# Up projection of a feed-forward block by seven block products instead of eight, gated activations through DRAM, and the down projection afterwards by token halves

## The chip, the cores and the metric

The kernel runs on one core of one Trainium2 chip. The metric is the device time of one execution in microseconds; the median of three runs of the kernel before is 1866.54 us (1864.61 to 1866.8).

## The reference

One layer of a hybrid causal decoder on a sequence of 1024 tokens with 1024 channels, all in float32. The token-mixing sub-layer (dilated attention and a convolution branch) and its output projection with a residual are left as they are. The change lies in the channel-mixing sub-layer:

```python
h = rms_norm(x, norm_ffn_pre)
u = h @ w_up                       # 1024 x 1024 times 1024 x 5632
u = causal_depthwise_conv(u, ffn_conv_w, ffn_conv_b)   # 3 taps along the tokens
u_gate, u_val = split(u, 2)        # 2816 channels each
f = gelu(u_gate) * u_val
y = f @ w_down                     # 1024 x 2816 times 2816 x 1024
x = x + rms_norm(y, norm_ffn_post)
```

## The kernel before, in words

All large products run on TensorE in a two-part form of float32: a value is split into a high part (`fp32r`, a ScalarE cast) and the remainder (a VectorE subtraction), and each product of two tiles is three matmuls into the same PSUM bank: high x high, high x low, low x high (`mm3`, lines 185 to 188). A matmul has a 128x128 stationary operand and 512 moving columns. Weights come from DRAM over the SP queue as 128x512 raw tiles (tag `wr`, three buffers) and are split by `split` (lines 166 and 167) into tiles `wh` and `wl` (seven buffers).

The engines work in order, each through its own list; a scheduler lays these lists out once, before the run, by a model of the times and the order of the program. Waits go through semaphores.

*Into the feed-forward part.* The output projection runs over eight token tiles in two halves (line 593). Each tile is normalised twice (with the residual between, lines 614 to 624) into rows `y`. When four tiles are there, `transposed` (lines 150 to 160) turns them on TensorE into `h2T[k, h]`: eight chunks k of 128 channels by 512 tokens, for the token half h, each as high and low part. The pool `d` has 31 buffers of 4 KB per partition for such tiles.

*Up.* `up(j)` (line 647) is called for j in 0 to 21. It makes 128 gate channels and 128 value channels of u: for both, for both token halves, over eight chunks, three matmuls, which is 2 x 2 x 8 x 3 = 96 matmuls of 512 columns into two PSUM tiles `pp` of two banks each. `conv3` (line 639) applies the three taps: one ScalarE activation and two VectorE operations of 1024 columns, reading PSUM (for j = 0 a copy in SBUF). Gelu (line 663), the product (664) and the split of f into high and low part (665, 666) follow; f stays in SBUF as `fT[j]`.

*Down.* Two blocks of f at a time are multiplied with the matching rows of `w_down` (line 687): for eight token tiles and two column halves, three matmuls for each block; the bank is then added by VectorE to an accumulator in SBUF (lines 704 and 706). The calls alternate with those of `up` (lines 711 to 716); the last call takes four blocks and ends each token tile with `finish` (line 671): the root mean square over the row, the scaling and the residual, and the store.

Of the kernel before, what the change touches and what calls it, by code (L numbers as in the profile page):

```python
# [18 lines left out]
P = 128  # L19
# [59 lines left out]
def trunk_kernel(ctx: ExitStack, tc: tile.TileContext, a, out):  # L79
# [5 lines left out]
    dpool = ctx.enter_context(tc.tile_pool(name="dpool", bufs=31))  # L85
# [44 lines left out]
    def rsqrt_of(ss, scale, eps, pool, tag, n=1):  # L130
# [17 lines left out]
        return y  # L148

# [51 lines left out]
    with ExitStack() as mix:  # L201
# [371 lines left out]
        h2T = {}  # L573
        with tc.tile_pool(name="res", bufs=1) as res:
# [18 lines left out]
            for h in range(2):  # L593
# [32 lines left out]
                for k in range(KC):  # L626
                    h2T[k, h] = dt(F32R, (P, 2, 512))
                transposed(h2, lambda k: (h2T[k, h][:, 0], h2T[k, h][:, 1]), ffn_g)


    with tc.tile_pool(name="ffn", bufs=1) as ffn:
        def h2_in(k, h):
            return h2T[k, h][:, 0], h2T[k, h][:, 1]

        acc = []
        fT = {}
        G = 2

        def conv3(ps, c, o, lo, hi):
            nc.scalar.activation(o[:, lo:hi], ps[:, lo:hi], AF.Identity, scale=ffn_w[:, c, 2:3], bias=ffn_b[:, c:c + 1])  # L640
            for k in (1, 0):
                d = 2 - k
                b = max(lo, d)
                nc.vector.scalar_tensor_tensor(o[:, b:hi], ps[:, b - d:hi - d], ffn_w[:, c, k:k + 1], o[:, b:hi],  # L644
                                               op0=ALU.mult, op1=ALU.add)

        def up(j, cuts=1):

            w = load_pair(a["w_up"][j], 4)
            pu = [pp_tile() for _ in range(2)]  # L650
            u = [ffn.tile([P, S], F32, tag="u", name="u", bufs=4) for _ in range(2)]
            fT[j] = fh, fl = dt(F32R), dt(F32R)
            n = S // cuts
            for lo in range(0, S, n):
                ts = slice(lo, lo + n)
                for c in range(2):
                    project(w, c, h2_in, pu[c], range(2 // cuts) if lo == 0 else (1,))
                    src = pu[c]
                    if j == 0:
                        src = ffn.tile([P, S], F32, tag="u", name="u", bufs=4)  # L660
                        (nc.vector.tensor_copy if c else nc.scalar.copy)(src, pu[c])
                    conv3(src, c * NF + j, u[c], lo, lo + n)
                nc.scalar.activation(u[0][:, ts], u[0][:, ts], AF.Gelu_apprx_tanh)
                nc.vector.tensor_mul(u[0][:, ts], u[0][:, ts], u[1][:, ts])
                nc.scalar.copy(fh[:, ts], u[0][:, ts])
                nc.vector.tensor_sub(fl[:, ts], u[0][:, ts], f(fh[:, ts]))

        post = ffn.tile([P, D], F32, name="post")
        nc.scalar.dma_start(post, a["norm_ffn_post"].to_broadcast((P, D)))

        def finish(T):
            o = acc[T]
            xr = ffn.tile([P, D], F32, tag="u", name="u", bufs=4)
            nc.sync.dma_start(xr, x2s[T * P:(T + 1) * P, :])
            ss = ffn.tile([P, 2], F32, tag="ss", name="ss", bufs=2)
            sq = pp_tile()
            cols = [slice(q * 512, q * 512 + 512) for q in range(2)]
            for q, cs in enumerate(cols):
                nc.scalar.activation(sq[:, cs], o[:, cs], AF.Square, accum_out=ss[:, q:q + 1])
                nc.vector.tensor_mul(o[:, cs], o[:, cs], post[:, cs])  # L680
# [6 lines left out]
        def down(ks, first=False, last=False):  # L687
            wd = {}
            for q in range(2):
                for n, k in enumerate(ks):  # L690
                    raw = wpool.tile([P, 512], F32, tag="wr", name="wr", bufs=3)
                    nc.sync.dma_start(raw, a["w_down"][k * P:(k + 1) * P, q * 512:(q + 1) * 512])
                    wd[k, q] = split(raw, (P, 512), *((ffn, "wd", 4) if n < G else (wpool, "w", 7)))
            for T in range(NT):
                ts = slice(T * P, (T + 1) * P)
                if first:
                    acc.append(dt() if T else ffn.tile([P, D], F32, name="acc0"))
                for q in range(2):
                    po = ps_tile()
                    for k in ks:  # L700
                        mm3(po, fT[k][0][:, ts], fT[k][1][:, ts], *wd[k, q], k == ks[0], k == ks[-1])
                    o = acc[T][:, q * 512:(q + 1) * 512]
                    if first:
                        nc.vector.tensor_copy(o, po)
                    else:
                        nc.vector.tensor_add(o, o, po)  # L706
                if last:
                    finish(T)

        groups = [list(range(k, k + G)) for k in range(0, NF, G)]  # L710
        for n, ks in enumerate(groups):
            for k in ks:
                up(k, 2 if k == NF - 1 else 1)
            if 0 < n < len(groups) - 1:
                down(groups[n - 1], first=n == 1)
        down(groups[-2] + groups[-1], last=True)


def _pairs(w, cols):
# [57 lines left out]
```

## Time and profile before

| | |
|---|---|
| median of three runs | 1866.54 us |
| the profiled execution, its own time | 1863.73 us |
| span of its instructions | 1862.0 us |
| TensorE busy | 1814.7 us (97%), 8392 matmuls |
| VectorE busy | 1134.3 us (61%) |
| ScalarE busy | 587.2 us (32%) |
| GpSimd busy | 57.1 us (3%) |
| moved by DMA | 143.86 MB, mean 77 GB/s |

The profile is that of one execution. PE is TensorE, PEld its weight loads, DVE VectorE, ACT ScalarE, POOL GpSimd, SP the engine whose queue issues most DMAs. Durations of matmuls are modelled and overlap: the pace is the distance from one start to the next. In a row of instruction groups stand line, engine, operation, `output<-inputs` by tile names, shapes, the count, then busy time and mean duration of one in ns, then the idle time of the engine in front of them and what ended it.

### The profile page before, as it was taken

The page shows a single profiled execution, that of the slowest core. Times are in us where ns is not written, and L with a number is a line of the kernel's source. Part 1 is how long each engine was busy: PE and PEld are TensorE (multiplying, and loading weights), DVE is VectorE, ACT ScalarE, POOL GpSimd, SP SyncE. Part 2 cuts the span into 40 slices and gives each one's busy share as a digit, 9 for nine tenths or more (in the row PEclk, how much of TensorE's full clock was granted, in tenths as well). Part 3 has the DMA queues.
Part 4 walks back from the last instruction along what each step waited for, and adds up shares of the span by engine and source line. Part 5 has one row for each costly group of instructions (what it writes and reads, how often), then busy time and mean ns, then how long its engine had stood idle before and what let it go on. Part 6 is the DMA issues. An engine that isn't in the chain of part 4 may idle for free.

```text
span 1862.0 us, 21816 instructions
## 1 busy us (share of the span) xinstructions
PE 1814.7 (97%) x8392; PEld 1524.2 (82%) x8392; DVE 1134.3 (61%) x1923; ACT 587.2 (32%) x1069; POOL 57.1 (3%) x83
## 2 busy tenths in 40 slices
PE   7899998999999999999999999999999999999997
PEld 5688898888888888888888887888888888888886
DVE  6249979258763769838654576555455545545548
ACT  6132343233313342223432344312221322222132
POOL 0000010011100000000000000000000000000000
PEclk9899999999999999999999999999999999999999
DMA  5312132122312222354231333211120211111114
GB/s 190 108 49 60 46 97 80 45 58 62 95 46 55 73 69 80 102 172 147 91 113 57 119 113 108 69 40 51 52 58 30 66 46 46 45 50 59 29 57 158
DMA packets 67079, 143.86 MB, mean 77 GB/s; under 512 B 9107, under 2 KB 11043, under 8 KB 66976
## 3 DMA queue, kind: packets, MB, share of 16 engines
q1 hardware_dynamic: 58176, 122.71, 21.4%
q0 software_dynamic: 5552, 16.19, 3.2%
q10 hardware_dynamic: 3248, 3.58, 0.6%
q8 instruction: 66, 1.08, 0.2%
q14 instruction: 37, 0.30, 0.0%
HBM read 119.23 MB, written 25.31 MB: 78 GB/s over the span
## 4 chain that ended last, share of the span: by engine, by line
PE 65%; issue 27%; DVE 2%; POOL 2%; DMA 2%; ACTq 1%; ACT 1%; SPq 0%; POOLq 0%; DVEq 0%
PE pp L186 16%; PE pp L188 16%; PE pp L187 16%; PE ps L186 2%; PE ps L188 2%; PE ps L187 2%; PE po L187 1%; PE po L186 1%; PE po L188 1%; PE pt L186 1%; PE pt L187 1%; PE pt L188 1%; ACTq L258 1%; POOL oscr L416 1%; POOL mscr L416 1%
## 5 line engine op out<-in xcount | busy, mean ns | idle before, releaser
L186 PE MATMUL pp<-d,wh 128*128 128x512 f32 x1792 | 702.3, 392 | 16.4 <-DVE d L332 15.2
L188 PE MATMUL pp<-d,wl 128*128 128x512 f32 x1792 | 701.9, 392 | 0.0
L187 PE MATMUL pp<-d,wh 128*128 128x512 f32 x1792 | 701.8, 392 | 0.0
L186 PEld LDWEIGHTS pp<-d,wh 128*128 128x128 f32 x1792 | 337.5, 188 | 86.9 <-issue 16.1
L188 PEld LDWEIGHTS pp<-d,wl 128*128 128x128 f32 x1792 | 337.6, 188 | 68.7
L187 PEld LDWEIGHTS pp<-d,wh 128*128 128x128 f32 x1792 | 337.7, 188 | 68.3
L167 DVE TENSOR_TENSOR wl<-wr,wh 128x512 fp32r<-128x512 f32 x283 | 194.2, 689 | 266.1 <-ACT wh L166 265.4
L271 DVE SCALAR_TENSOR_TENSOR acc<-cin,conv_w,acc 128x1024 f32<-128x1024 f32 x240 | 305.2, 1281 | 3.1
L166 ACT CAST wh<-wr 128x512 fp32r<-128x512 f32 x283 | 175.0, 622 | 344.9 <-PE pp L187 234.4
L644 DVE SCALAR_TENSOR_TENSOR u<-pp,ffn_w,u 128x1023 f32<-128x1023 f32 (+2 forms) x88 | 108.4, 1232 | 81.8 <-ACT u L640 80.7
L166 ACT CAST wdh<-wr 128x512 fp32r<-128x512 f32 x40 | 24.8, 622 | 184.8 <-PE ps L188 150.0
L325 PE MATMUL pp<-wh,d 128*128 128x512 f32 x192 | 79.6, 415 | 3.0 <-DVE d L332 3.0
L326 PE MATMUL pp<-wl,d 128*128 128x512 f32 x192 | 78.9, 411 | 0.0
L327 PE MATMUL pp<-wh,d 128*128 128x512 f32 x192 | 77.4, 408 | 0.0
L640 ACT ACTIVATE u<-pp,ffn_b,ffn_w 128x1024 f32<-128x1024 f32 (+1 forms) x44 | 51.3, 1166 | 77.6 <-PE pp L188 77.6
L706 DVE TENSOR_TENSOR d<-d,ps 128x512 f32<-128x512 f32 x63 | 43.2, 686 | 43.6 <-PE ps L188 43.6
L186 PE MATMUL ps<-wdh,d 128*128 128x512 f32 x160 | 62.2, 389 | 0.0
L187 PE MATMUL ps<-wdl,d 128*128 128x512 f32 x160 | 62.2, 389 | 0.0
L188 PE MATMUL ps<-wdh,d 128*128 128x512 f32 x160 | 62.2, 389 | 0.0
L380 ACT ACTIVATE pe<-sn,ml 128x128 f32<-128x128 f32 (+1 forms) x96 | 42.5, 445 | 52.7 <-DVE ml L377 52.4
L325 PEld LDWEIGHTS pp<-wh,d 128*128 128x128 f32 x192 | 53.1, 277 | 7.1 <-issue 4.0
L327 PEld LDWEIGHTS pp<-wh,d 128*128 128x128 f32 x192 | 52.9, 277 | 3.6 <-issue 0.9
(268 smaller groups left out, 2035.6 us busy)
## 6 DMA issues: line engine op xcount, KB each, us to landing
wr<-in_w_up_dram SPq DMA_DIRECT2D x88, 256.0 KB, 2.8
wr<-in_w_v_dram SPq DMA_DIRECT2D x48, 256.0 KB, 2.8
wr<-in_w_qk_dram SPq DMA_DIRECT2D x48, 256.0 KB, 2.7
wr<-in_w_down_dram SPq DMA_DIRECT2D x44, 256.0 KB, 2.9
wr<-in_w_glu_dram SPq DMA_DIRECT2D x32, 256.0 KB, 2.7
wr<-in_w_gate_dram SPq DMA_DIRECT2D x32, 256.0 KB, 3.0
ld<-oscr SPq DMA_DIRECT2D x8, 768.0 KB, 5.6
d<-in_x_dram SPq DMA_DIRECT2D x8, 512.0 KB, 5.8
```

Of the source, the lines that this page charges most:

```text
L166: nc.scalar.copy(hi, raw)
L167: nc.vector.tensor_sub(lo, raw, f(hi))
L186: nc.tensor.matmul(ps, lh, rh, start=first, stop=False)
L187: nc.tensor.matmul(ps, lh, rl, start=False, stop=False)
L188: nc.tensor.matmul(ps, ll, rh, start=False, stop=last)
L271: nc.vector.scalar_tensor_tensor(acc, cin[:, k:k + S], conv_w[:, m, k:k + 1], acc, op0=ALU.mult, op1=ALU.add)
L325: nc.tensor.matmul(ps, hTh[k][:, sl], wh, start=k == 0, stop=False)
L326: nc.tensor.matmul(ps, hTh[k][:, sl], wl, start=False, stop=False)
L327: nc.tensor.matmul(ps, hTl[k][:, sl], wh, start=False, stop=k == KC - 1)
L640: nc.scalar.activation(o[:, lo:hi], ps[:, lo:hi], AF.Identity, scale=ffn_w[:, c, 2:3], bias=ffn_b[:, c:c + 1])
L644: nc.vector.scalar_tensor_tensor(o[:, b:hi], ps[:, b - d:hi - d], ffn_w[:, c, k:k + 1], o[:, b:hi], op0=ALU.mult, op1=ALU.add)
L706: nc.vector.tensor_add(o, o, po)
```

## The change

*Operands.* The chunks k and k+4 of the normalised rows form the upper and lower half of the input (B11 and B21 for the first 512 tokens, B12 and B22 for the second). When the second half has been transposed, `strassen_rows` forms for each of four k the sums T1 = B12 - B11, T2 = B22 - T1, T3 = B22 - B12 and T4 = B21 - T2 and splits each into high and low part. B11 to B22 and T1 to T4 are 32 tiles; the pool `d` gets 32 buffers. The weights of a block are stored as four quadrants of 128 rows by 512 columns (gate and value channels by upper and lower half of the input: A11, A12, A21, A22), and GpSimd forms S1 = A21 + A22, S2 = S1 - A11, S3 = A11 - A21 and S4 = A12 - S2 of them.

*Up.* Blocks 0 and 1 run as before in eight products each (`up_plain`, first the first token half of both, then the second). Blocks 2 to 21 run as seven products of 12 matmuls (class `Seven`), in two banks of which partial sums are copied from one to the other by ScalarE (bank 1 to 2 in `fifth`, bank 2 to 1 in `second`). The loop begins the next block (`Seven(j + 1)`, `fifth`) between the products of the current one. The taps read the gate and value rows from SBUF. f is split as before, in place, and written to DRAM (`fscr`) by two DMAs per block on GpSimd's queue.

*Down.* After all up blocks, `down(0)` and `down(1)` take one token half each: four token tiles by two column halves stand in all eight PSUM banks over all 22 blocks, so nothing is added in SBUF. Each step loads f and two halves of the rows of `w_down`, so the weights are loaded and split twice. The last three blocks are taken tile by tile, with `finish` after each tile, which first copies the two banks to SBUF.

```diff
-    dpool = ctx.enter_context(tc.tile_pool(name="dpool", bufs=31))
+    dpool = ctx.enter_context(tc.tile_pool(name="dpool", bufs=32))
+    def strassen_rows(b11, b21, pt12, pt22, gain12, gain22, temp, make):
+        def parts(x):
+            t = make()
+            nc.scalar.copy(t[:, 0], x)
+            nc.vector.tensor_sub(t[:, 1], x, f(t[:, 0]))
+            return t
+        b12, b22 = temp("x12"), temp("x22")
+        nc.scalar.activation(b12, pt12, AF.Copy, scale=gain12)
+        nc.scalar.activation(b22, pt22, AF.Copy, scale=gain22)
+        out = {"B22": parts(b22), "B12": parts(b12)}
+        t1, t3, t2 = temp("x1"), temp("x3"), temp("x2")
+        nc.gpsimd.tensor_sub(t3, b22, b12)
+        nc.vector.tensor_sub(t1, b12, f(b11[:, 0]))
+        nc.vector.tensor_sub(t1, t1, f(b11[:, 1]))
+        out["T1"] = parts(t1)
+        out["T3"] = parts(t3)
+        nc.vector.tensor_sub(t2, b22, t1)
+        out["T2"] = parts(t2)
+        nc.vector.tensor_sub(t2, f(b21[:, 0]), t2)
+        nc.vector.tensor_add(t2, t2, f(b21[:, 1]))
+        return out, lambda: parts(t2)
...
+                temps = {"x12": ("xr", 0), "x22": ("xr", 1), "x1": ("oc", 0), "x2": ("oc", 1)}
+                for k in range(4):
+                    pair = [ps_tile((P, 4, P), tag) for tag in ("pt", "po")]
...
+                    wide = {"xr": nat2("xr", 2), "oc": nat2("oc", 1)}
...
+        def u_tile():
+            return ffn.tile([P, S], F32, tag="u", name="u", bufs=6)
+        def conv3(src, c):
+            o = u_tile()
+            nc.scalar.activation(o, src, AF.Identity, scale=ffn_w[:, c, 2:3], bias=ffn_b[:, c:c + 1])
             for k in (1, 0):
...
+        def gated(j, gate, val):
+            og, ov = conv3(gate, j), conv3(val, NF + j)
+            nc.scalar.activation(og, og, AF.Gelu_apprx_tanh)
+            nc.vector.tensor_mul(og, og, ov)
+            nc.scalar.copy(ov.bitcast(F32R), og)
+            nc.vector.tensor_sub(og.bitcast(F32R), og, ov)
+            for n, src in enumerate((ov, og)):
+                nc.gpsimd.dma_start(fscr[j, :, :, n, :].rearrange("h p c -> p h c"),
+                                    src.rearrange("p (h c) -> p h c", h=2))
+        def raw_tile(early=False):
+            if early:
+                return wpool.tile([P, 512], F32, tag="wr", name="wr", bufs=3)
+            return ffn.tile([P, 512], F32, tag="wq", name="wq", bufs=5)
...
+        def product(ps, w, x, first, last, open_=False):
+            for k in range(4):
+                cs = slice(k * P, k * P + P)
+                xh, xl = X[x, k][:, 0], X[x, k][:, 1]
+                for n, (wp, xp) in enumerate(((w[0], xh), (w[0], xl), (w[1], xh))):
+                    nc.tensor.matmul(ps, wp[:, cs], xp, ...)
+        def up_plain(js):
+            us = {(j, c): u_tile() for j in js for c in range(2)}
+            pps = {c: pp_tile() for c in range(2)}
+            for h in range(2):
+                for n, j in enumerate(js):
+                    for c in range(2):
+                        ps = pps[c][:, h * 512:(h + 1) * 512] if n == 0 else ps_tile(tag="ps")
+                        for kh in range(2):
+                            product(ps, wsplit(quadrant(j, 2 * c + kh)), ("B11", "B21", "B12", "B22")[2 * h + kh], kh == 0, kh == 1)
+                        dst = us[j, c][:, h * 512:(h + 1) * 512]
+                        (nc.vector.tensor_copy if c else nc.scalar.copy)(dst, ps)
+            for j in js:
+                gated(j, us[j, 0], us[j, 1])
+        class Seven:
+            def __init__(self, j):
+                self.a11, self.a21, self.a22, self.a12 = (quadrant(j, q) for q in (0, 2, 3, 1))
+                self.s = [ffn.tile([P, 512], F32, tag="ws", name="ws", bufs=4) for _ in range(4)]
+                s1, s2, s3, s4 = self.s
+                nc.gpsimd.tensor_add(s1, self.a21, self.a22)
+                nc.gpsimd.tensor_sub(s2, s1, self.a11)
+                nc.gpsimd.tensor_sub(s3, self.a11, self.a21)
+                nc.gpsimd.tensor_sub(s4, self.a12, s2)
+                both = pp_tile()
+                self.b1, self.b2 = both[:, 0:512], both[:, 512:1024]
+                self.gate, self.val = u_tile(), u_tile()
+                product(self.b1, wsplit(self.a11), "B11", True, False, True)
+            def fifth(self):
+                product(self.b2, wsplit(self.s[0]), "T1", True, False, True)
+                nc.scalar.copy(self.gate[:, 512:1024], self.b2)
+                nc.scalar.copy(self.b2, self.b1)
+            def second(self):
+                product(self.b1, wsplit(self.a12), "B21", False, False, True)
+                nc.scalar.copy(self.gate[:, 0:512], self.b1)
+                product(self.b2, wsplit(self.s[1]), "T2", False, False, True)
+                nc.scalar.copy(self.b1, self.b2)
+            def seventh(self):
+                product(self.b2, wsplit(self.s[2]), "T3", False, False, True)
+                nc.vector.tensor_add(self.val[:, 512:1024], self.b2, self.gate[:, 512:1024])
+            def last(self):
+                product(self.b1, wsplit(self.s[3]), "B22", False, False, True)
+                nc.vector.tensor_add(self.gate[:, 512:1024], self.b1, self.gate[:, 512:1024])
+                product(self.b2, wsplit(self.a22), "T4", False, False, True)
+                nc.scalar.copy(self.val[:, 0:512], self.b2)
+                gated(self.j, self.gate, self.val)
+        up_plain((0, 1))
+        now = Seven(2)
+        now.fifth()
+        for j in range(2, NF):
+            now.second()
+            then = Seven(j + 1) if j + 1 < NF else None
+            now.seventh()
+            if then:
+                then.fifth()
+            now.last()
+            now = then
...
+        def finish(T, banks):
+            xr = u_tile()
             nc.sync.dma_start(xr, x2s[T * P:(T + 1) * P, :])
+            o = u_tile()
+            nc.scalar.copy(o[:, cols[0]], banks[0])
+            nc.vector.tensor_copy(o[:, cols[1]], banks[1])
...
+        def down(h, late=3):
+            wide = [pp_tile() for _ in range(2)]
+            banks = [[w[:, cs] for cs in cols] for w in wide]
+            banks += [[ps_tile(tag="ps") for _ in range(2)], [ps_tile(tag=tag) for tag in ("pt", "po")]]
+            def load(k):
+                ft = dt(F32R, (P, 2, 512))
+                nc.sync.dma_start(f(ft), fscr[k, h])
+                w = []
+                for cs in cols:
+                    raw = raw_tile()
+                    nc.sync.dma_start(raw, a["w_down"][k * P:(k + 1) * P, cs])
+                    w.append(wsplit(raw))
+                return ft, w
+            def step(t, k, ft, w):
+                ts = slice(t * P, (t + 1) * P)
+                for q in range(2):
+                    mm3(banks[t][q], ft[:, 0, ts], ft[:, 1, ts], *w[q], k == 0, k == NF - 1)
+            order = (3, 2, 0, 1)
+            for k in range(NF - late):
+                fw = load(k)
+                for t in order:
+                    step(t, k, *fw)
+            fws = [(k, load(k)) for k in range(NF - late, NF)]
+            for t in order:
+                for k, fw in fws:
+                    step(t, k, *fw)
+                finish(4 * h + t, banks[t])
+        down(0)
+        down(1)
```

`wsplit` is `split` with the seven buffers `wh` and `wl`; `quadrant` loads one quadrant over the SP queue, for blocks 0 and 1 into the three `wr` buffers, later into the five `wq` buffers.

## Rows read from the trace of the kernel before

**Rows 1.** The page: the span and the busy time of each engine

```profile
span 1862.0 us, 21816 instructions
PE 1814.7 (97%) x8392; PEld 1524.2 (82%) x8392; DVE 1134.3 (61%) x1923; ACT 587.2 (32%) x1069; POOL 57.1 (3%) x83
```

**Rows 2.** Busy time of each engine in stretches of the span

```profile
core 0: us, PE busy (x) PEld busy (x) DVE busy (x) ACT busy (x) POOL busy (x), PEclk, DMA share, GB/s
20.00:41.00 21.00, 21.00 (x115) 17.69 (x114) 15.69 (x32) 12.50 (x22) 0.00 (x0) 1.00 0.50 150
...
1200.00:1500.00 300.00, 300.00 (x1325) 248.51 (x1324) 155.93 (x185) 73.08 (x89) 0.00 (x0) 1.00 0.16 47
...
1850.00:1862.00 12.00, 0.65 (x3) 0.19 (x2) 8.33 (x31) 0.72 (x2) 0.00 (x0) 0.64 0.35 131
```

**Rows 3.** Timeline of TensorE: start, duration, line, operation, tiles

```profile
1127.56 0.48 PE L186 MATMUL pp<-d,wh 128*128 128x512 f32 x1
...
1135.62 0.39 PE L188 MATMUL pp<-d,wl 128*128 128x512 f32 x1
...
1138.34 0.39 PE L188 MATMUL pp<-d,wl 128*128 128x512 f32 x1
1138.57 0.27 PE L156 MATMUL ps<-ident,y 128*128 128x128 f32 x1
1138.68 0.27 PE L156 MATMUL po<-ident,y 128*128 128x128 f32 x1
...
1850.27 0.39 PE L188 MATMUL pt<-wh,d 128*128 128x512 f32 x1
```

**Rows 4.** Groups of VectorE instructions by line and shape

```profile
L167 DVE TENSOR_TENSOR wl<-wr,wh 128x512 fp32r<-128x512 f32 x283 | 194.2, 689 | 266.1 <-ACT wh L166 265.4
...
L666 DVE TENSOR_TENSOR d<-u,d 128x1024 fp32r<-128x1024 f32 x21 | 25.7, 1223 | 12.5 <-ACT d L665 12.5
L664 DVE TENSOR_TENSOR u<-u 128x1024 f32<-128x1024 f32 x21 | 25.7, 1222 | 1.6 <-ACT u L663 1.3
...
L704 DVE COPY d<-ps 128x512 f32<-128x512 f32 x7 | 4.8, 689 | 9.3 <-PE ps L188 9.3
...
L644 DVE SCALAR_TENSOR_TENSOR u<-u,ffn_w 128x1023 f32<-128x1023 f32 x2 | 2.5, 1282 | 0.4 <-ACT u L640 0.4
```

**Rows 5.** Groups of ScalarE instructions by line and shape

```profile
L166 ACT CAST wh<-wr 128x512 fp32r<-128x512 f32 x283 | 175.0, 622 | 344.9 <-PE pp L187 234.4 <-PE pp L327 51.5 <-DMA wr<-in_w_up_dram 15.2
...
L663 ACT ACTIVATE u<-u 128x1024 f32<-128x1024 f32 x21 | 22.3, 1061 | 54.5 <-DVE u L644 54.5
L665 ACT CAST d<-u 128x1024 fp32r<-128x1024 f32 x21 | 22.1, 1051 | 83.6 <-DVE u L664 83.6
...
L679 ACT ACTIVATE pp<-d 128x512 f32<-128x512 f32 x14 | 8.4, 602 | 26.4 <-DVE d L706 18.6 <-DVE rfy L147 4.7 <-DVE rft L137 1.9
L611 ACT COPY oc<-pp 128x512 f32<-128x512 f32 x14 | 7.5, 590 | 19.4 <-PE pp L188 12.4 <-DVE y L618 7.0
...
L640 ACT ACTIVATE u<-u,ffn_b,ffn_w 128x1024 f32<-128x1024 f32 x2 | 2.4, 1240 | 0.0
```

**Rows 6.** Groups of GpSimd instructions

```profile
L621 POOL DMA_DIRECT2D x2s<-xr x8 | 4.7, 593 | 311.0 <-ACT y L620 244.8 <-DVE xr L619 48.2 <-DVE rpy L147 18.0
...
masks.py:199 POOL TENSOR_SCALAR_AFFINE_SELECT ident<-ident 128x128 f32<-128x128 f32 x1 | 0.3, 287 | 0.1
```

**Rows 7.** Timeline of VectorE: the last normalised rows, and the first transposed chunk after

```profile
1137.13 0.75 DVE L624 TENSOR_SCALAR y<-xr,rpy 128x1024 f32<-128x1024 f32 x1
1140.04 0.75 DVE L160 SCALAR_TENSOR_TENSOR d<-ps,ffn_g,d 128x512 fp32r<-128x512 f32 x1 [2.15 <-ACT d L159]
```

**Rows 8.** DMA: a stretch at the start, and issues with KB and us to landing

```profile
4.00:6.00 2.00, 0.00 (x0) 0.00 (x0) 0.54 (x5) 1.37 (x3) 0.00 (x0) 1.00 1.03 360
...
wr<-in_w_down_dram SPq DMA_DIRECT2D x44, 256.0 KB, 2.9
...
u<-x2s SPq DMA_DIRECT2D x8, 512.0 KB, 4.4
```

More of the change, by code (lines that the diff above doesn't have):

```diff
@@ L572, in trunk_kernel @@
         x2s = dram.tile([S, D], F32, name="x2s")
-        h2T = {}
+        h2T, X = {}, {}
         with tc.tile_pool(name="res", bufs=1) as res:
@@ L625, in trunk_kernel @@
                     h2.append(y)
-                for k in range(KC):
-                    h2T[k, h] = dt(F32R, (P, 2, 512))
-                transposed(h2, lambda k: (h2T[k, h][:, 0], h2T[k, h][:, 1]), ffn_g)
-    with tc.tile_pool(name="ffn", bufs=1) as ffn:
[L632 to L640, printed above, removed]
+                if h == 0:
+                    for k in range(KC):
+                        h2T[k] = dt(F32R, (P, 2, 512))
+                    transposed(h2, lambda k: (h2T[k][:, 0], h2T[k][:, 1]), ffn_g)
+                    continue
@@ L645, in conv3 @@
                                                op0=ALU.mult, op1=ALU.add)
[L647 to L666, printed above, removed]
@@ L668, in trunk_kernel @@
-        post = ffn.tile([P, D], F32, name="post")
+            return o
+        def gated(j, gate, val):
[7 more added lines that the diff above has]
+                                    src.rearrange("p (h c) -> p h c", h=2))
@@ new lines, in raw_tile, with quadrant, wsplit @@
+        def raw_tile(early=False):
+            if early:
+                return wpool.tile([P, 512], F32, tag="wr", name="wr", bufs=3)
+            return ffn.tile([P, 512], F32, tag="wq", name="wq", bufs=5)
+        def quadrant(j, q):
+            raw = raw_tile(j < 2)
+            nc.sync.dma_start(raw, a["w_up"][j, q])
+            return raw
+        def wsplit(raw):
+            return split(raw, (P, 512), wpool, "w", 7)
+        def product(ps, w, x, first, last, open_=False):
[3 more added lines that the diff above has]
+                for n, (wp, xp) in enumerate(((w[0], xh), (w[0], xl), (w[1], xh))):
+                    nc.tensor.matmul(ps, wp[:, cs], xp, start=first and k == 0 and n == 0,
+                                     stop=last and k == 3 and n == 2, skip_group_check=open_)
@@ L669, in trunk_kernel @@
+        up_plain((0, 1))
[9 more added lines that the diff above has]
+            now = then
+        post = dt()
         nc.scalar.dma_start(post, a["norm_ffn_post"].to_broadcast((P, D)))
-        def finish(T):
-            o = acc[T]
-            xr = ffn.tile([P, D], F32, tag="u", name="u", bufs=4)
+        cols = [slice(q * 512, q * 512 + 512) for q in range(2)]
@@ L685, in finish @@
                 nc.sync.dma_start(out[T * P:(T + 1) * P, cs], o[:, cs])
[L687 to L697, printed above, removed]
-                for q in range(2):
[L699 to L708, printed above, removed]
@@ L726, in _pairs, with _quads @@
     return np.ascontiguousarray(np.stack(out).reshape(len(cols), K // 256, P, 2, 256))
+def _quads(w, cols):
+    blk = w.reshape(2, 4, P, w.shape[1] // P, P)
+    out = [blk[:, :, :, c].transpose(0, 2, 1, 3).reshape(2, P, 512) for pair in cols for c in pair]
+    return np.ascontiguousarray(np.stack(out).reshape(len(cols), 4, P, 512))
 _OUT = ((1, S, D), "float32")
@@ L751, in _layout @@
         "w_out": i["w_out"][0],
-        "w_up": _pairs(i["w_up"][0], [(j, NF + j) for j in range(NF)]),
+        "w_up": _quads(i["w_up"][0], [(j, NF + j) for j in range(NF)]),
         "w_down": i["w_down"][0],
```

35 lines of the change are left out of this document (23 added, 12 removed).

## The prediction

> **What bounds the kernel now.** I read the page's busy shares first: TensorE is busy for 97% of a span of 1862.0 us, VectorE for 61%, ScalarE for 32%, GpSimd for 3% [rows 1]. A share over the whole span can hide stages with another limit, so the table by stages comes next [rows 2]. From 1200 to 1500 us, in the middle of the feed-forward part, TensorE is busy for 300.00 of 300 us at granted clock 1.00, the 2.4 GHz level, with VectorE at 156 us and ScalarE at 73 us. So this part is bounded by the number of matmuls and their pace, and no wait ends last in it. The pace comes from start to start, since the listed durations overlap: 12 steps from 1135.62 to 1138.34 us are 0.2267 us each [rows 3]. As a cross-check, the part has 22 x 96 up matmuls and 22 x 8 x 2 x 3 = 1056 down matmuls, 3168 in all; at 0.2267 us that is 718.2 us, and the first and last of them start 722.7 us apart [rows 3], with 32 transposes of 0.11 us (3.5 us) between. TensorE loses about a microsecond there.
>
> **What is removed.** Blocks 2 to 21 take seven products of 12 matmuls instead of 96 matmuls: 84. That is 20 x 12 = 240 fewer; blocks 0 and 1 and the down projection keep their counts. 240 x 0.2267 = **-54.4 us**, as long as TensorE is never kept waiting. Everything below asks where it is.
>
> **The loop over blocks 2 to 21.** A block now lasts 84 x 0.2267 = 19.04 us on TensorE, and the other engines must fit in that. VectorE: 7 weight splits at 0.69, four convolution steps at 1.28, multiply and subtract at 1.22 each, two bank reads at 0.69: 4.8 + 5.1 + 2.4 + 1.4 = 13.8 us, 72% [rows 4]. ScalarE: 7 casts at 0.62, five bank copies at 0.60, two 1.24 convolution starts, gelu 1.06, cast 1.05: 4.4 + 3.0 + 2.5 + 2.1 = 12.0 us, 63% [rows 5]. The two copies from bank to bank have no row; reads from a bank and writes to one both stand near 0.60, so I take that. GpSimd gets four additions of 128x512, which no row shows. Below, they cost what VectorE needs, 0.69 us [rows 4]; above, four times the 0.287 us that GpSimd's select on 128x128 took [rows 6], 1.15 us. I take 1.15 us, since that row is GpSimd's own. With two DMA issues at 0.59 us [rows 6] GpSimd has 5.8 us per block. All three fit. The nearest stage for such a load is 20 to 41 us, where VectorE was 75% and ScalarE 60% busy and TensorE stayed at 21.00 of 21 us [rows 2]; so I take **0**, with the two queues below as the upper ends.
>
> What is queued: in GpSimd's queue the additions of a later block can stand behind the writes of f, which wait for the gated product's last subtraction. Five raw buffers let three weights of the next block arrive before that, so its first sum can be formed early; no charge. Weight splits run up to six products (16 us) ahead through seven buffers. The shortest slack is TensorE's on ScalarE: bank 2 is copied to bank 1 after the second product of `second`, and only one product, 12 x 0.2267 = 2.7 us, lies ahead of the one that overwrites bank 2. The writes of f, 23 MB, and their reads lie beside this and cost nothing unless GpSimd's queue stands.
>
> **The entry.** The last normalised rows are there at 1137.13 + 0.75 = 1137.9 us [rows 7]. TensorE then has its 96 first-half matmuls (21.8 us from 1127.6 us), which need none of them, and the 3.5 us of transposes, until about 1153; it reaches chunk 3 of the next product 2 us later, at 1155. For that chunk the source buffers come free (two of them) when chunk 1's T1 and T2 are formed. That is 18 to 20 VectorE steps of 0.69 us [rows 4] after the first transposed chunk (today its first split runs from 1140.04 us [rows 7]), so 1153 to 1154, and 2 us for the evacuation and split. I charge 1 us (0 to 8, where ScalarE's turns add up). Next comes VectorE's debt. From 1138 us it has 44 steps of the operand sums (30.4 us), 9 splits (6.2), 4 bank copies (2.8), the gating of blocks 0 and 1 (2 x 7.6) and 4 splits for block 2 (2.8): 57 us, until 1195. TensorE wants the last of these at 1138.6 + 10.9 + 3.5 + 21.8 + 3 x 2.7 = 1183. If the gating goes first, it waits 12 us; if the splits do, 0. I take 6. Entry: **+7** (0 to 20).
>
> **Down projection.** 1056 matmuls as before: 0. Each step of 24 matmuls (5.44 us) now needs 512 KB of f and 512 KB of weights, 193 GB/s. At 4 to 6 us the loads ran at 360 GB/s with several in flight [rows 8]; one alone lands in 2.9 us (256 KB) or 4.4 us (512 KB), and five raw and seven split buffers let some five steps be ahead: hidden. The 44 added splits are 1.4 us of VectorE per 5.44. Handing over from up to down: tiles 3 and 2 start in banks that stand free, **+1** (0 to 4). Between the halves, six of the seven weight buffers serve the last three steps, and VectorE owes finishing work: about 5.2 us for a token tile (three steps at 0.69, two at 0.7, some 1.7 in small ones) against 18 x 0.2267 = 4.1 us of TensorE, so the next splits come late: **+3** (0 to 6). The end: today 11.7 us pass from the last matmul's start to the span's end [rows 3]; four tiles of 1.1 us lag make it **+2** (0 to 4).
>
> **Sum.** -54.4 + 7 + 0 + 1 + 3 + 2 = -41.4 us. The profiled execution took 1863.7 us, span and 1.7 us around it, so 1822.3; the median of the runs shown lies 2.8 us above it, which gives **1825 us**. With every wait at its lower end it is 1812; with every wait above 0 at its upper end (20 + 4 + 6 + 4) 1846.
>
> **A rule that speaks against it.** Today GpSimd does nothing in the loop (0.00 us in rows 2), so no row shows its additions beside VectorE. Most VectorE work in the new loop reads two SBUF tensors, the convolution too, since its source moves from PSUM to SBUF. The Trainium skill (SBUF — State Buffer, "Who interferes with whom") says that a VectorE instruction with two SBUF inputs and a GpSimd instruction that reads SBUF exclude each other: whichever comes second waits until the first is done. No run here shows that yet; by it the sum would be the first rival's.
>
> **The rivals.**
> 1. *GpSimd's additions hold VectorE.* Four at 1.15 us on top of 13.8 make 18.4 of 19.04 us. VectorE still fits, but has 3% left, and one held turn per block lands ahead of a bank read or a split with little slack: 1.15 x 20 = +23 us, **1848 us**. For: VectorE's queue is in order and the plan of the instructions was laid without such holds. Against: splits are made up to 16 us ahead, bank reads have 5.4 us. Chance 0.18. From 1.31 us per addition on, VectorE would bound the loop. (The Trainium skill, GPSIMD Engine Reference, "Performance versus the Vector engine", has a two-input operation of GpSimd take about 1.96 times VectorE's time; as an estimate from that page 1.35 us, which no run here shows yet and which would put this rival just over that point.)
> 2. *Slower than before: the bank 2 to bank 1 copy stands behind a waiting ScalarE queue.* Today ScalarE stands for 54.5/21 = 2.6 us ahead of each gelu, waiting for VectorE's convolution [rows 5]. If, in every block, the copy is queued behind such a gelu, TensorE waits for 1.2 (a convolution start) + 2.6 + 1.06 + 0.60 - 2.7 = 2.8 us a block, 55 us in all: 1825 + 55 = **1880 us**. Decided by ScalarE's order: the gain is gone from 41.4/20 = 2.1 us per block on. Against: gelu is due some 5 us after the block before has its last product (0.6 + 0.7 + 1.24 + 2 x 1.28), the copy 5.4 us after it, so gelu should be through or just so. Chance 0.10.
> 3. *The entry at its upper end*, with the halves' change too: 20 + 6 in place of 7 + 3, **1841 us**; chance 0.10. A long wait there could also cost clock: in the idle last 12 us the granted clock fell to 0.64 on average [rows 2].
>
> That the change does not do what it says can be excluded for its count: the matmuls are written out, 84 a block.
>
> **How the numbers follow.** My forecast gets 0.62, spread from 1812 to about 1838, and the likeliest value is the sum's, 1825. The range 1812 to 1850 takes in rivals 1 and 3 and leaves out rival 2 and what lies below the floor. A measurement can tell about 0.2% (3.7 us) from no change, so "same" is 1863 to 1870. All but rival 2, and mixtures of 1 and 2, are faster: 0.87; same 0.03; slower 0.10.
>
> **What would show it.** Right: 84 matmuls per block at 0.2267 us, TensorE busy in every window of the loop, ScalarE near 63% and VectorE near 72% there, a few waits of TensorE between 1150 and 1200 us, one between the two halves, and an end of some 13 to 14 us after the last matmul. GpSimd's additions near 1.15 us, VectorE's durations as before. Rival 1: VectorE's 128x512 steps become longer or stand idle while GpSimd works. Rival 2: TensorE's matmuls of T3 wait for ScalarE's copy. The forecast is wrong if TensorE idles over 0.5 us per block in the loop, or if down steps wait for f or for weights.

## The result: 1.35% slower, and the profile after

| | before | after |
|---|---|---|
| median of four runs each, same chip | 1866.4 us | 1891.16 us |
| lowest to highest | 1864.61 to 1866.8 | 1889.86 to 1892.74 |
| ratio, 95% interval | | 1.0135, 1.0117 to 1.0152 |
| span of the profiled execution | 1862.0 us | 1891.0 us |

The forecast was 1825 us, faster, with a range of 1812 to 1850 us. The kernel got slower instead, and the result lies outside the range.

The page of the kernel after, the lines that answer to [rows 1]:

```profile
span 1891.0 us, 22339 instructions
PE 1782.0 (94%) x8152; PEld 1488.4 (79%) x8152; DVE 1187.2 (63%) x1956; ACT 720.7 (38%) x1312; POOL 217.7 (12%) x211
```

The 240 matmuls are gone (8392 to 8152) and TensorE is busy for 32.7 us less, but the span grew by 29.0. So TensorE waits more than it saves. Where it waits shows in the busy time by stretches, with the columns of [rows 2]:

```profile
1150.00:1160.00 10.00, 6.38 (x38) 4.75 (x36) 9.28 (x13) 6.93 (x13) 4.65 (x3) 1.00 0.07 26
1160.00:1170.00 10.00, 0.00 (x0) 0.00 (x0) 9.21 (x14) 4.48 (x8) 1.49 (x1) 0.54 0.00 0
1170.00:1180.00 10.00, 0.00 (x0) 0.00 (x0) 9.18 (x16) 4.59 (x9) 0.00 (x0) 0.50 0.00 0
1180.00:1190.00 10.00, 5.23 (x16) 4.22 (x17) 4.85 (x9) 2.70 (x5) 0.46 (x1) 0.59 0.40 130
...
1300.00:1400.00 100.00, 92.87 (x397) 75.32 (x396) 68.81 (x71) 51.95 (x75) 33.39 (x26) 0.98 0.27 90
...
1740.00:1879.00 139.00, 139.00 (x614) 115.08 (x614) 56.76 (x142) 41.58 (x80) 0.00 (x0) 1.00 0.38 122
1880.00:1891.00 11.00, 0.07 (x1) 0.00 (x0) 7.51 (x29) 2.03 (x5) 0.00 (x0) 0.70 0.42 156
```

Three things are to be seen. Between 1157 and 1185 us TensorE does nothing; VectorE is 92% busy from 1160 to 1180 us. In the loop over the blocks it is busy for 93% where it had 100%. In the down projection it is full, and the end behind the last matmul is as short as before. The waits of TensorE, in all and by what released them, put names to the first two:

```profile
engine line waited for: us in total, times, longest us
PE pp L729 <- DVE u L779: 31.9, 19, 1.8
PE pp L729 <- ACT u L743: 27.8, 1, 27.8
```

L729 is the matmul of `product`. L779 is VectorE's addition in `seventh`, which reads bank 2. L743 is the copy of a bank to `us` in `up_plain`.

**The ledger.** From its restart at 1184.77 us to the end TensorE has 96 + 1680 + 1056 = 2832 matmuls, 642.0 us at 0.2267. The last one starts at 1879.69, so 695.1 us passed: **53.1 us lost**. The up part began 2.9 us later than in [rows 3] (1130.45 for 1127.56 us; the up parts of the kernels below began between 1123.9 and 1132.6 us, so this is variation ahead of it). The end takes 11.3 us where it took 11.7. In sum: 2.9 - 54.4 + 27.8 (the one wait) + 53.1 - 0.4 = 29.0, the whole difference of the spans. The prediction had charged 7 and 0 for the two large terms.

**The loop.** The starts of gelu (ScalarE, L701), one in each block, give a block's period in the kernel after:

```profile
1283.96 1.06 ACT L701 ACTIVATE u<-u 128x1024 f32<-128x1024 f32 x1
1306.73 1.06 ACT L701 ACTIVATE u<-u 128x1024 f32<-128x1024 f32 x1
1327.85 1.06 ACT L701 ACTIVATE u<-u 128x1024 f32<-128x1024 f32 x1
1348.98 1.06 ACT L701 ACTIVATE u<-u 128x1024 f32<-128x1024 f32 x1
```

The periods are 22.8, 21.1 and 21.1 us, and so on, nearly always in this pattern; over 8 blocks from 1240.10 to 1413.94 us the mean is 21.73, where 84 matmuls are 19.04. The timeline around one of the 19 waits shows what TensorE stands for:

```profile
1401.64 1.29 POOL L759 TENSOR_TENSOR ws<-wq 128x512 f32<-128x512 f32 x1 [2.36 <-DVE wl L193]
...
1402.13 1.88 DVE L704 TENSOR_TENSOR u<-u 128x1024 fp32r<-128x1024 f32 x1 [0.57 <-ACT u L703]
...
1402.50 0.39 PE L729 MATMUL pp<-d,wl 128*128 128x512 f32 x1
...
1403.93 0.68 DVE L779 TENSOR_TENSOR u<-pp,u 128x512 f32<-128x512 f32 x1
...
1404.67 0.73 PE L729 MATMUL pp<-d,wh 128*128 128x512 f32 x2 [1.78 <-DVE u L779]
```

TensorE ends the product with T3 into bank 2. VectorE's read of bank 2 stands behind L704, which takes 1.88 us here while GpSimd forms S3. Only when the read is done does TensorE begin the product with B22, **into bank 1**. Nothing in the data asks for that. The two banks are halves of one tile `pp`, and the reading here is that the waits are made per tile; the first experiment tests it. And the scheduler put no product between: per block it runs B21, T4 of the block before, T2, B11 and T1 of the next, T3, B22.

**The entry.** Around the restart at 1184.77 us:

```profile
1183.41 0.69 DVE L157 TENSOR_TENSOR d<-oc,d 128x512 fp32r<-128x512 f32 x1 [0.68 <-ACT d L156]
1184.13 0.58 ACT L743 COPY u<-pp 128x512 f32<-128x512 f32 x1 [0.76 <-DVE d L157]
...
1184.24 1.28 SPq L717 DMA_DIRECT2D wq<-in_w_up_dram  x3
...
1184.77 0.79 PE L729 MATMUL pp<-d,wh 128*128 128x512 f32 x1 [27.82 <-ACT u L743]
```

L156 and L157 split the last operand sum (`parts` in `strassen_rows`). The copy of block 0's first half follows it at once, and TensorE follows the copy. The data of the copy have nothing to do with that split. Its destination, a tile `u`, lies in the pool `ffn`, which opens when the pool `res` with the sums' temporaries is closed, so the reading is that it takes over their memory (tested below, in the run with other memory for the copies). TensorE's next product, block 0's second half, goes into the other half of the tile that is being copied, so it waits too, though the parts of B12 and B22 of the first chunks are ready: VectorE made those of chunk 0 by 1152.7 us.

VectorE's groups of the loop (1240 to 1560 us), for [rows 4], and then two of GpSimd's four sums there, for [rows 6]:

```profile
L193 DVE TENSOR_TENSOR wl<-wq,wh 128x512 fp32r<-128x512 f32 x44 | 46.6, 1060 | 12.5 <-ACT wh L192 12.3
...
L704 DVE TENSOR_TENSOR u<-u 128x1024 fp32r<-128x1024 f32 x15 | 28.2, 1878 | 8.6 <-ACT u L703 8.6
...
L779 DVE TENSOR_TENSOR u<-pp,u 128x512 f32<-128x512 f32 x15 | 10.2, 677 | 0.0
...
L758 POOL TENSOR_TENSOR ws<-ws,wq 128x512 f32<-128x512 f32 x15 | 33.1, 2209 | 36.4 <-issue 33.9 <-DVE wl L193 2.5
...
L759 POOL TENSOR_TENSOR ws<-wq 128x512 f32<-128x512 f32 x15 | 19.4, 1292 | 35.5 <-DVE wl L193 35.5
```

The subtraction that had 1223 ns [rows 4] takes 1878; weight splits from `wq` take 1060 for 689. GpSimd's addition takes 1.29 us, or 2.2 where it meets VectorE.

### The profile page after: what moved, and what is told of

Same layout as the page of the kernel before. It is cut to its first block, busy times and chain, and to the rows that moved or that the text cites. A ratio compares the mean times of both kernels' runs of the same rounds, so it can differ in the third digit from the quotient of the medians.

```text
span 1891.0 us, 22339 instructions
## 1 busy us (share of the span) xinstructions
PE 1782.0 (94%) x8152; PEld 1488.4 (79%) x8152; DVE 1187.2 (63%) x1956; ACT 720.7 (38%) x1312; POOL 217.7 (12%) x211
## 5 line engine op out<-in xcount | busy, mean ns | idle before, releaser
L212 PE MATMUL pp<-d,wh 128*128 128x512 f32 x1088 | 429.8, 395 | 15.9 <-DVE d L358 15.6
L729 PE MATMUL pp<-d,wh 128*128 128x512 f32 x1184 | 377.2, 400 | 61.7 <-DVE u L779 31.9
L214 PE MATMUL pp<-d,wl 128*128 128x512 f32 x1088 | 428.8, 394 | 0.0
L213 PE MATMUL pp<-d,wh 128*128 128x512 f32 x1088 | 428.7, 394 | 0.0
L729 PEld LDWEIGHTS pp<-d,wh 128*128 128x128 f32 x1184 | 226.5, 193 | 118.1 <-DVE u L779 40.0
L193 DVE TENSOR_TENSOR wl<-wr,wh 128x512 fp32r<-128x512 f32 x207 | 142.2, 691 | 162.5 <-ACT wh L192 162.1
L729 PE MATMUL pp<-d,wl 128*128 128x512 f32 x592 | 235.4, 398 | 0.0
L192 ACT CAST wh<-wr 128x512 fp32r<-128x512 f32 x207 | 127.7, 621 | 279.4 <-PE pp L213 164.3
L193 DVE TENSOR_TENSOR wl<-wq,wh 128x512 fp32r<-128x512 f32 x148 | 122.2, 832 | 148.0 <-ACT wh L192 146.6
L192 ACT CAST wh<-wq 128x512 fp32r<-128x512 f32 x148 | 91.8, 623 | 221.3 <-PE pp L214 119.3
L694 DVE SCALAR_TENSOR_TENSOR u<-u,ffn_w 128x1023 f32<-128x1023 f32 x88 | 113.7, 1292 | 53.0 <-ACT u L691 53.0
L729 PEld LDWEIGHTS pp<-d,wl 128*128 128x128 f32 x592 | 114.3, 193 | 24.6
L192 ACT CAST wh<-ws 128x512 fp32r<-128x512 f32 x80 | 49.3, 618 | 119.8 <-PE pp L729 119.8
L212 PE MATMUL pp<-wh,d 128*128 128x512 f32 x232 | 90.2, 391 | 0.7 <-ACT oc L637 0.7
L213 PE MATMUL pp<-wl,d 128*128 128x512 f32 x232 | 90.4, 390 | 0.0
L214 PE MATMUL pp<-wh,d 128*128 128x512 f32 x232 | 90.4, 390 | 0.0
L351 PE MATMUL pp<-wh,d 128*128 128x512 f32 x192 | 79.5, 415 | 3.0 <-DVE d L358 3.0
L352 PE MATMUL pp<-wl,d 128*128 128x512 f32 x192 | 78.3, 408 | 0.0
```

Source lines behind the costliest of these rows:

```text
L192: nc.scalar.copy(hi, raw)
L193: nc.vector.tensor_sub(lo, raw, f(hi))
L212: nc.tensor.matmul(ps, lh, rh, start=first, stop=False)
L213: nc.tensor.matmul(ps, lh, rl, start=False, stop=False)
L214: nc.tensor.matmul(ps, ll, rh, start=False, stop=last)
L351: nc.tensor.matmul(ps, hTh[k][:, sl], wh, start=k == 0, stop=False)
```

## The experiments

Theory A: the loop loses its time because products into one bank wait for reads of the other (one tile), and what VectorE is held by GpSimd only lengthens that wait. Rival B: GpSimd's hold on VectorE is the cause, and the shared tile is by the way. For the entry, theory C: the shared tile and the memory keep TensorE; rival D: VectorE's operand sums set its end whatever TensorE waits for by name.

### Each bank a tile of its own

```diff
-                both = pp_tile()
-                self.b1, self.b2 = both[:, 0:512], both[:, 512:1024]
+                self.b1, self.b2 = ps_tile(tag="ps"), ps_tile(tag=("pt", "po")[j % 2])
...
-            order = (3, 2, 0, 1)
+            order = (0, 1, 2, 3)
```

The loop alternates over four banks as before; only the tiles are cut otherwise (and the down projection starts with the tiles that are now free).

> The two partial-sum banks of a block become two one-bank tiles in place of one two-bank tile. Theory A (the matmuls wait for a read of the OTHER bank, because the two banks are one tile): the waits of TensorE for the VectorE read of the T3 product (1.7 us, 19 times) disappear, a block takes 19.0 to 19.5 us instead of 21.7, and the time falls by 40 to 52 us to 1839 to 1851 us. Theory B (VectorE is held up by GpSimd's additions, so its reads come late): the held turns reach TensorE at another place, a block stays above 20.5 us and the time above 1868 us.

Measured: 1841.82 us, ratio 0.9886 (0.9866 to 0.9906) to the kernel before. Gelu, a stretch of the loop, and the step from T3 (into `po`) to B22 (into `ps`):

```profile
1273.65 1.06 ACT L701 ACTIVATE u<-u 128x1024 f32<-128x1024 f32 x1
1292.69 1.07 ACT L701 ACTIVATE u<-u 128x1024 f32<-128x1024 f32 x1
1311.74 1.06 ACT L701 ACTIVATE u<-u 128x1024 f32<-128x1024 f32 x1
```

```profile
1300.00:1400.00 100.00, 100.00 (x443) 82.81 (x442) 76.20 (x80) 58.57 (x84) 35.88 (x33) 1.00 0.36 119
```

```profile
1321.64 0.62 PE L729 MATMUL ps<-d,wh 128*128 128x512 f32 x2
...
1321.84 0.69 DVE L778 TENSOR_TENSOR u<-po,u 128x512 f32<-128x512 f32 x1 [1.55 <-PE po L729]
```

A block lasts 19.04 us, the count times the pace, and TensorE is full. From its restart (1181.48 us) to the end it loses 646.1 - 642.0 = 4.1 us where it lost 53.1. The waits for the read of bank 2 are gone; the one of 27.9 us in the entry stands. B22 still follows T3 at once, and now it starts before the read of T3's bank (L778) does: with a tile of its own, the matmul doesn't wait for the other bank. That is theory A.

### No sums on GpSimd, with the two-bank tile kept

```diff
-                self.s = [ffn.tile([P, 512], F32, tag="ws", name="ws", bufs=4) for _ in range(4)]
-                s1, s2, s3, s4 = self.s
-                nc.gpsimd.tensor_add(s1, self.a21, self.a22)
...
+                self.s = [self.a21, self.a22, self.a21, self.a12]
```

S1 to S4 are left out; raw quadrants stand in for them.

> Leaves out GpSimd's four sums of weight quadrants per block (the products use unsummed quadrants, as many splits as before); the two banks stay one tile. Theory A: the product S4 x B22 still has to wait for the read that follows the T3 product directly (0.3 us to start, 0.68 us long), so 0.8 to 1.1 us per block are left and the time falls by only 10 to 30 us, to 1861 to 1881 us. Theory B: the wait falls below 0.3 us per block, a block takes 19.1 to 19.4 us and the time falls to about 1840 us.

Measured: 1860.98 us in a single run. TensorE's wait for the same read, and the subtraction of f without GpSimd beside it:

```profile
PE pp L729 <- DVE u L774: 14.9, 19, 0.8
```

```profile
L704 DVE TENSOR_TENSOR u<-u 128x1024 fp32r<-128x1024 f32 x16 | 19.6, 1226 | 4.1 <-ACT u L703 4.1
```

A block lasts 20.15 us, and from the restart (1179.48 us) to the end of the last matmul (started at 1847.45) it loses 668.2 - 642.0 = 26.2 us. So with the shared tile, the read alone costs 22.1 us (26.2 - 4.1), and GpSimd's sums add 26.9 (53.1 - 26.2). The time lies at the lower edge of A's range and some 21 us above B's.

### Both at once

Own banks and no sums: the two diffs above together.

> One-bank tiles, and GpSimd's four weight sums per block left out. Theory A: with one-bank tiles the reads have a product of 2.7 us to hide behind, so GpSimd's hold on VectorE costs nothing any more: a block at 19.04 us with and without the sums, time within 3 us of the one-bank kernel (1839 to 1845 us). Theory B: the sums still cost something, and the time falls by more than 5 us below it.

Measured: 1841.99 us in a single run, as with the sums (1841.82); the loss is 4.0 for 4.1. VectorE's steps there and in the run with own banks and sums differ as they did: f's subtraction takes 1226 ns without the sums, and with them

```profile
L694 DVE SCALAR_TENSOR_TENSOR u<-u,ffn_w 128x1022 f32<-128x1022 f32 x34 | 59.1, 1738 | 0.0
...
L704 DVE TENSOR_TENSOR u<-u 128x1024 fp32r<-128x1024 f32 x17 | 33.9, 1994 | 8.8 <-ACT u L703 8.8
```

B falls as a cause of its own: VectorE is held just as long (1994 ns, and the convolution step 1738 for 1278), and it costs nothing once a read has a product to hide behind.

### The entry: banks of the two plain blocks cut by token half

```diff
-            pps = {c: pp_tile() for c in range(2)}
+            pps = {h: pp_tile() for h in range(2)}
...
-                        ps = pps[c][:, h * 512:(h + 1) * 512] if n == 0 else ps_tile(tag="ps")
+                        ps = pps[h][:, c * 512:(c + 1) * 512] if n == 0 else ps_tile(tag=("ps", "ps", "pt", "po")[2 * h + c])
```

> Only the banks of blocks 0 and 1 change: each token half has its own tile, so the second half's products need no copy of the first half's. Theory A: the wait of 27.8 us for a copy, which itself waits for the last operand sum to release memory, goes; what is left is the wait for the operands of chunk 3, ready at about 1177 us instead of 1184.8, so the time falls by 7 to 12 us to 1879 to 1884 us. Rival (VectorE's operand sums set the end of the entry anyway, and the copies and the loads of block 2 start with it): same within 3 us, 1888 to 1894.

Measured: 1887.34 us, ratio 1.0126 (1.011 to 1.0143) where the kernel after has 1.0135 (1.0117 to 1.0152): no difference clear of the intervals, and a time between the two forecasts, nearly the rival's. The wait came apart instead of going:

```profile
PE pp L729 <- ACT d L156: 9.8, 4, 4.8
PE pp L729 <- DVE d L157: 3.9, 4, 1.9
PE pp L729 <- ACT pp L769: 3.8, 1, 3.8
```

TensorE now follows the operands chunk by chunk, and the granted clock is 0.66 and 0.52 in the two stretches from 1160 to 1180 us. The operands that VectorE and ScalarE make (L156, L157) set these pieces, as D has it. But the edit does not free blocks 0 and 1 of the shared tile: the gate and the value bank of a token half are now the two halves of one. By the counts of matmuls, block 0's value products of both halves (48 into `pp`) come last, from 1189.8 us on, though 24 of them, those of the first half, need none of the new operands. So C is not excluded by this run.

### Own banks in the loop and in the entry

The first and the last diff together.

> Both edits. If the two waits are independent, their gains add: 1829 to 1843 us, faster than the kernel before the change by 23 to 37 us. If the loop only hides what the entry loses (the engines catch up in it), the sum is smaller than the two gains, by up to 8 us.

Measured: 1841.55 us, ratio 0.9884 (0.9863 to 0.9905): what the loop's banks alone gave. Block 3's gelu starts at 1235.60 us, there at 1235.57; the up part began 1.6 us later here (1128.70 for 1127.10), so no more than that was gained. The time lies within the range for gains that add, but only because that range reaches up to no gain at all.

### B12 and B22 of the first three chunks formed ahead of the sums

On top of the last one, `strassen_rows` is cut in two, and the parts of B12 and B22 are made first, so that the second half of both plain blocks need not wait for the sums:

```diff
+                for k in range(3):
+                    b_phase(k)
+                t_phase(0)
+                b_phase(3)
+                for k in range(1, 4):
+                    t_phase(k)
```

> Both bank edits, and the parts of B12 and B22 are formed for three of the four chunks before any T sum. If the entry's end is set by when TensorE gets the operands of the second half, they are ready some 10 us earlier and the time falls by 6 to 12 us, to 1830 to 1836 us. If it is set by the last operand sum (near 1184 us), after which the memory of the feed-forward part comes free and the copies, the gating and the loads of block 2 start, the time stays within 3 us of 1841.5.

Measured: 1841.78 us, ratio 0.988 (0.9863 to 0.9897), no gain. TensorE now works through 1160 to 1170 us (9.69 us busy) and stands later:

```profile
PE pp L734 <- ACT u L748: 10.5, 1, 10.5
PE ps L734 <- ACT pt L773: 6.4, 1, 6.4
```

The first of these two waits ends where the last sum is split (1179.6 us). By the counts it is again the shared tile: the 48 matmuls into `pp` from 1180.2 us on are block 0's value products of both halves, held by the copy of its gate rows (L748) out of the other bank. The second wait (until 1210.4 us) is for a copy from bank to bank in `fifth`, behind a gelu in ScalarE's list, while VectorE, with the gating of blocks 0 and 1 to do, is busy for 10.00 of the 10 us from 1205 to 1215. So TensorE had more of its work done when the sums ended, and lost the lead again behind what the other engines still owed. No kernel here gives blocks 0 and 1 a tile per bank, so what the tile costs in the entry stays open.

### Half of the operand sums, and then the copies to other memory

On top of own banks in the loop; T2 and T4 are left out with their splits (B22 and B21 stand in), 20 of VectorE's steps, 13.8 us at 0.69:

```diff
-        nc.vector.tensor_sub(t2, b22, t1)
-        out["T2"] = parts(t2)
-        nc.vector.tensor_sub(t2, f(b21[:, 0]), t2)
-        nc.vector.tensor_add(t2, t2, f(b21[:, 1]))
-        return out, lambda: parts(t2)
+        return out
```

> One-bank tiles; the sums T2 and T4 and their splits are left out (B22 and B21 stand in for them), so 20 of 44 VectorE steps of the entry go (5 of 11 per chunk). If the last operand sum sets the entry's end: it comes near 1168 us instead of 1184, TensorE's wait for the copy falls from 27.9 to 10 to 15 us, time 1824 to 1831 us. If something else sets it (weights of blocks 0 to 2, GpSimd): within 4 us of 1842.

The second kernel also takes the copies' destinations from the pool `d`, which waits for no temporaries: `us = {(j, c): dt() ...}`.

> As the kernel with half the sums, and the rows of blocks 0 and 1 go to tiles of the pool d (free because of the sums left out), so their copies need not wait for the end of the sums. If the memory of the copies was the last wait of TensorE: the wait for the copy is gone, TensorE waits chunk by chunk for operands instead (5 to 10 us together), time 4 to 9 us below the kernel with half the sums. If it was only the messenger of VectorE's debt, the same within 2 us.

Measured, a single run each: 1827.43 and 1825.39 us. The wait in the first, then in the second, and the copies there:

```profile
PE pp L725 <- ACT u L739: 13.3, 1, 13.3
```

```profile
PE pp L725 <- DVE d L739: 11.3, 1, 11.3
```

```profile
1164.49 0.69 DVE L739 COPY d<-pp 128x512 f32<-128x512 f32 x1
...
1165.65 0.58 ACT L739 COPY d<-pp 128x512 f32<-128x512 f32 x1
...
1166.28 0.69 DVE L157 TENSOR_TENSOR d<-x,d 128x512 fp32r<-128x512 f32 x1
```

Half of the sums take 14.6 us of the wait and 14.4 of the time: the debt of VectorE's sums, as D has it, sets the end. With other memory the copies run ahead of the last split, so the memory did hold them; but that takes only 2.0 us more off the wait. (The time falls by 2.0 us too, which two single runs can't tell from nothing: four runs of the kernel with own banks lie 5.4 us apart.) TensorE then waits for a copy that stands among the sums in VectorE's list, and it waits for it through the tile that both token halves share. So the sums' length is shown as a cause; how the rest divides between VectorE's order and the tile is not.

### A third block in eight products

The sums can't be left out, but TensorE can be given work beside them. On top of the kernel with B12 and B22 first, block 2 is run in eight products too; block 0 keeps both halves in its PSUM tiles and its taps read them there:

```diff
-        up_plain((0, 1))
-        now = Seven(2)
+        up_plain((0, 1, 2))
+        now = Seven(3)
```

> Edit: the kernel of the run before (own banks, B12 and B22 formed first), with three blocks in eight products instead of two. Block 0 keeps both token halves in its two-bank PSUM tiles and its taps read them there; blocks 1 and 2 are copied out as before. Theory: the entry's end is set by the last operand sum, about 1184 us, and TensorE idles some 25 us ahead of it only because it has no product that needs none of the sums. The third block gives it 48 more first-half matmuls (10.9 us), and block 0's second half (10.9 us) needs neither the sums nor the memory that the copies wait for. After the last sum 20 x 84 matmuls become 19 x 84: 19.0 us less, given back in part by 8 more weight splits that VectorE does ahead of it (8 x 0.69 = 5.5 us). So 13 to 19 us under the run before: 1823 to 1829 us. Rival: VectorE's later debt (three gatings instead of two, 7.6 us more) or the late weight loads keep TensorE waiting as long after the sums as it idled ahead of them; then the 2.7 us of the twelve added matmuls remain, 1842 to 1845 us.

Measured: 1828.76 us against 1864.92 before, ratio 0.9802 (0.9786 to 0.9819): **the fastest kernel here that computes all of it**, 0.8% ahead of the one it was made from (ratios 0.9802 and 0.988). The expectation was 13 to 19 us; the medians differ by 13.0. In the entry:

```profile
1160.00:1170.00 10.00, 10.00 (x48) 8.09 (x47) 9.24 (x15) 6.07 (x12) 1.69 (x1) 1.00 0.02 5
1170.00:1180.00 10.00, 10.00 (x45) 8.07 (x43) 9.90 (x16) 5.32 (x11) 2.90 (x1) 1.00 0.42 127
1180.00:1190.00 10.00, 0.17 (x1) 0.00 (x0) 9.14 (x15) 3.89 (x8) 0.00 (x0) 0.63 0.11 27
```

```profile
1191.70 0.69 DVE L654 TENSOR_TENSOR d<-oc,d 128x512 fp32r<-128x512 f32 x1 [0.68 <-ACT d L653]
```

```profile
PE ps L734 <- ACT u L749: 12.9, 1, 12.9
```

TensorE is full until 1180 us. The last sum is split at 1192.4 us where it was 1184.1, since VectorE makes 12 weight splits ahead of it where the kernel after has 3 (9 at 0.69 are 6.2 of the 8.3 us; the up part also began 2.1 us later, 1132.58 for 1130.45 us); so 12.9 us of waiting are left, again for a copy behind the last sum.

## Why the prediction was wrong, and where it was right

**Matmuls, right.** 84 per block at 0.2267 us are 19.04 us, and with own banks a block takes just that. VectorE and ScalarE fit: 76% and 59% there, forecast 72% and 63%.

**The loop, wrong; the larger failure.** The step charged 0, with VectorE's share of a block and queue leads as the reason. It checked whether VectorE had the time, not whether TensorE had something to do meanwhile. TensorE waits 1.7 us a block (31.9 us in 19 waits), over the 0.5 that the prediction had named as the sign of being wrong. The slack that failed is "bank reads have 5.4 us" under rival 1: that is two products of 2.7 us, as there would be if only the *same bank* had to wait. The wait is on the tile, and in the order the scheduler chose the next product into that tile follows T3 at once, so the slack was nothing. The text named another pair as the shortest ("bank 2 is copied to bank 1"), a wait that comes to 1.0 us once (L775). The Trainium skill (PSUM — Partial Sum Buffer, "Summary: rules for kernel authors") advises reading one bank while matmuls write another, with the semaphore guarding the bank; the run with own banks agrees, at 19.04 us a block, and the kernel after guards two banks as one.

**GpSimd's additions, right in kind and wrong in place.** 1.29 us each for a forecast of 1.15. Rival 1 (23 us) is real: the sums add 26.9 us in the kernel after. But it works through the shared tile alone; without it the same hold costs nothing. So the argument against it (splits lead, reads have slack) holds for separate banks. The Trainium skill (SBUF — State Buffer, "Who interferes with whom") gives the hold its rule, and the trace agrees: 1226 ns without GpSimd's sums, 1878 with them. From the factor of 1.96 in the Trainium skill (GPSIMD Engine Reference, "Performance versus the Vector engine") came the estimate of 1.35 us for an addition; the trace has 1.28 to 1.30 where VectorE is out of the way.

**The entry, wrong.** The debt was sized about right for its part ahead of the gating: the sums and splits end at 1184.1 us, and the text had TensorE want the last of them at 1183. What failed is that TensorE was to spend the time until then on the second halves of blocks 0 and 1 (96 matmuls, 21.8 us), so that +7 sufficed. It could not: their banks were held for copies that came only behind the last sum, and TensorE stood for 27.8 us. (21.8 and the charged 6 make the same 27.8 by chance: the 6 was for gating ahead of splits, and no such wait is in the trace.) Three kernels that cut the banks otherwise or formed operands earlier gained little or nothing: TensorE then waited for the operands, or for ScalarE's and VectorE's work behind the sums. Only fewer sums (14.4 us) or more work ahead of them (13.0) moved the end. What the tile of two banks adds in the entry stays open.

**The clock, a rival's aside, came true.** The entry's wait was noted as a danger to it; the granted clock there is 0.50 to 0.59, and the first products after it run at about half pace.

**Down projection, right, and a little better.** No wait on f or on the weights, TensorE 139.00 of 139 us from 1740 on; the 3 us forecast between the halves are not there (from 1613 us on the only wait is one of 0.8, on L779), and an end of 11.3 us for 13 to 14.

**Rival 2** (ScalarE's queue, 55 us) gave the right sign by another mechanism: no such wait is in the trace. The price of 2.7 us a block happens to be near its 2.8.

Of the 26.9 us that GpSimd's sums add, 17.0 are the longer waits (31.9 - 14.9). Most of the rest can be put to the pace after them (last section): seven blocks between 1240 and 1611 us last 22.7 to 22.8 us instead of 21.1, 11.3 us in all, an estimate somewhat above the 9.9 that are left.

## What to carry to other kernels

A wait is made for the object that the framework tracks, not for the bytes or the bank: before a slack is counted in products, ask which tile the next write belongs to and in what order the scheduler may put it. A tile per bank cost nothing in the loop and gave back 49 us here. When an engine owes a long debt at a stage's entry, moving waits about inside it can gain nothing, as in three kernels here; shorten the debt or give the waiting engine work that needs none of it, and look at whose memory a new pool takes over.

## What the runs showed of the hardware that was not expected

After a wait of 1.8 us in each block TensorE sometimes loses pace for some 4 us. In the stretch from 1295 to 1300 us its granted clock is 0.73. The timeline of its matmuls there, in the kernel after:

```profile
1295.80 0.73 PE L729 MATMUL pp<-d,wh 128*128 128x512 f32 x2 [1.78 <-DVE u L779]
...
1297.29 1.01 PE L729 MATMUL pp<-d,wh 128*128 128x512 f32 x2
1298.10 0.63 PE L729 MATMUL pp<-d,wl 128*128 128x512 f32 x1
1298.53 1.05 PE L729 MATMUL pp<-d,wh 128*128 128x512 f32 x2
```

Three matmuls take 1.24 us from 1297.29 to 1298.53, 0.41 each, near the pace of the 1.2 GHz level, and 0.23 again from 1301 us on. About every third block has this, and lasts 22.8 us instead of 21.1; waits of 0.8 us, in the kernel without sums, never brought it (20.1 to 20.2 us in all blocks of the loop until 1578 us). A short wait repeated so costs more than its length: 1.78 us of waiting became 2.08 in most blocks and 3.7 in the others.
